# Rows of the output projection parked in DRAM, two more weight buffers, and row sums on GpSimd

## The chip, the cores and the metric

One NeuronCore of a Trainium2 chip runs the whole kernel; times are device microseconds of that core, median of three runs. TensorE (PE) multiplies, VectorE (DVE), ScalarE (ACT) and GpSimd (POOL) do the rest, and the queue of SyncE (SP) issues nearly all DMAs.

## The reference

A block of one layer over 512 tokens of width 1024: three mixers (gated linear attention, stick-breaking attention, pooling) share one input and one output projection, then a mixture of 32 experts (two per token, all in one group of eight), then a gated input embedding and a last norm.

```
h = x + mix @ w_out
h = h + hier_moe(rmsnorm(h), ...)          # 32 experts of 3 x 1 MB, 2 per token
gate = sigmoid(rmsnorm(h, g3) @ ple_gate_w + ple_gate_b)
h = h + gate * (p @ ple_proj_w)
return rmsnorm(h, final_norm_g)
```

## The kernel before

The 512 tokens are four tiles of 128. After the mixers, `h1[t]` holds the rows of the output projection (x plus mix times w_out), one buffer of 128x1024 floats for each tile, in the pool `hp`; they stay in SBUF to the end. Routing makes for every token two places in lists of experts; the normed rows go to `tnd` in DRAM, and each of 16 steps gathers the rows of two experts (`xg`), turns them, multiplies by gate and up weights (`gate_up`, line 997), then by the down weights (`down`, line 1029), and scatters the results to `yd` in DRAM by an indirect DMA of GpSimd. Only the last step, 15, stays on the chip: `scatter` adds its rows to `h1` by a matmul with a one-hot matrix (line 1051) and an addition on VectorE (line 1053).

Weights come in 96 units of 1 MB, issued in a fixed order by SP (`load_units`, line 691) into buffers that a list `ring` hands out: 20 in all, each given back when its step has used it. A load also waits for the one issued three before it (`AHEAD`). SP, PE and, from step 14 on, ACT and DVE run in the order in which the code is written; GpSimd's order is set by the scheduler of the framework.

Behind the units SP issues, for the tail: the returned rows of tile 0 (`load_y(0)`, both experts' rows, 1 MB), four pieces of the gate weights (`gate_load`, 4 MB), `load_y(1)`, a broadcast row of 0.5 MB, `load_y(2)`, another such row, `load_y(3)`. Then, for each tile t:

- `add_y(t)` (line 1164): two additions of 128x1024 of the returned rows to `h1[t]`, and `scatter` of step 15's; together `sums(t)`.
- `turn(t)` (line 1221): eight transposes on PE, copies by ACT (1223) and DVE (1224), as a high and a low part.
- `gate(t)`: 48 matmuls of 128x512 (line 1242) with the gate weights, which `gate_hi` (ACT, 1071) and `gate_lo` (DVE, 1075) have split in 16 pieces into a high and a low part.
- `rms(t)`: squares on ACT (1229), two tiny sums on DVE (1208, 1210), and a power on GpSimd (`rsp`, line 63).
- `finish(t)`: DVE 1252 (which needs `rsp`), ACT sigmoid 1253, DVE 1254, 1255, 1257, ACT 1256, and the output DMA.

ACT and DVE hold the copies of `turn(t+1)` behind the first half of `finish(t)`. 32 small steps of the embedding's product (`ple`, line 724) are spread over the expert steps by the table `PLE`, the last twelve over the tail by `PLE_LAST`.

Of the kernel before, what the change touches and what calls it, by code (L numbers as in the profile page):

```python
# [27 lines left out]

FILL = (8, 3, 0, 1, 0, 1, 0, 1, 0, 1, 1, 1, 4, 2, 2, 2, 9)

PLE = (5, 1, 1, 1, 1, 1, 1, 1, 1, 1, 1, 1, 1, 1, 2)
PLE_LAST = (4, 4, 4)
AHEAD = 3
NR, NL = 4, 9
CLEAR = (7, 8, 9, 10)
# [53 lines left out]
def mixers(ctx, tc, A, K, dbg):  # L89
# [360 lines left out]
    sbctx.close()  # L450
    pctx.close()
    hp = ctx.enter_context(tc.tile_pool(name="hp", bufs=1, side="left"))
    h1 = K["h1"] = [hp.tile([P, D], F32, name=f"h1_{t}") for t in range(NT)]
    for t in range(NT):
        nc.sync.dma_start(h1[t], A["x"][t * P:(t + 1) * P, :])
    parts = (step for t in range(NT) for hf in range(2) for step in out_proj(nc, K, mixh, mixl, hf, t, WO_EARLY))
# [157 lines left out]
def ffn(ctx, tc, A, K, mixh, mixl, out, dbg, stage):  # L614
# [67 lines left out]

    slab, loads = {}, []

    def load_units(m=96):

        while ring and m and len(slab) < 96:
            n, m = len(slab), m - 1
            n = n - n % 6 + (0, 3, 1, 4, 2, 5)[n % 6]
            slab[n] = unit(F32, [P, 2048])  # L690
            loads.append(nc.sync.dma_start(slab[n], A["w_exp"][n // 3, n % 3]).ins)
            if len(loads) > AHEAD:
                tc.add_manual_dep(loads[-1], loads[-1 - AHEAD].name,
                                  mybir.DependencyInfo(mybir.DependencyClass.Sync, mybir.DependencyReason.DATA))
# [20 lines left out]
    def ple_steps():  # L715

        pT, pW = pl_in
        for j in range(8):
            t, hf = j // 2, j % 2
            p = ps("pe", "sc" if j < 5 else "gu")  # L720
            for c in range(2):
                for k in range(2):
                    n = hf * 512 + c * 256
                    PE.matmul(p[:, c * 256:c * 256 + 256], pT[:, k * S + t * P:k * S + (t + 1) * P], pW[:, k, n:n + 256],  # L724
                              start=(k == 0), stop=(k == 1))
                    if c == k == 1:
                        kept.append((t, hf, p))
                        ple_out()
                    yield
# [14 lines left out]
    V.tensor_copy(cm.rearrange("p a b -> p (a b)"), cmf)  # L744
    V.tensor_tensor(rw, rw, g2c[:, :, None].to_broadcast([P, KC, 36]), ALU.mult)
    tnd = dram.tile([S, D], F32, name="tnd")
    Ab = mw.tile([P, NT, 32], BF, name="Ab")
    pr_ = cw.tile([P, 448], F32, name="pr", tag="cmf")
    posA = pr_[:, :128].rearrange("p (t e) -> p t e", t=NT)
# [87 lines left out]
    def weights(t, g8, e8, id2, c0):  # L837
# [22 lines left out]
        V.tensor_copy(rt(1), pe(c0))  # L860
        V.tensor_tensor(rt(2), pe(c0), rt(1), ALU.subtract)

    chosen = {}
    halves = [(t, hf) for t in range(NT) for hf in range(2)]

# [7 lines left out]
    with tc.manual_schedule(engines={mybir.EngineType.PE}):  # L873
        for hf in range(2):
            part(hf, 0, WO_LATE[:2])
        for n in range(len(halves) - 1):
            part(halves[n][1], halves[n][0], WO_LATE[2:] if n < 2 else WO_LATE)
            if n >= 2:
                logits(*halves[n - 2])
            if n >= 1:  # L880
                route_in(*halves[n - 1])
            if n >= 2:
                t, hf = halves[n - 2]
                if hf:
                    run(route(t))
                    load_units(2)
                    if t > 0:
                        position(t - 1)
                        run(weights(t - 1, *chosen[t - 1]))
                elif t > 1:  # L890
                    position(t - 1)
                    run(weights(t - 1, *chosen[t - 1]))
        with tc.manual_schedule(engines={mybir.EngineType.DVE}):
            last_part = out_proj(nc, K, mixh, mixl, 1, NT - 1, WO_LATE)
            run(last_part, 2)
            logits(NT - 2, 1)
            steps = [route(t) for t in (NT - 2, NT - 1)]
            run(steps[0], 7)
            run(last_part)
        ring.extend(((mix, "m3"), (mix, "m1"), (mix, "m2")))  # L900
        for hf in range(2):
            route_in(NT - 1, hf)
        logits(NT - 1, 0)
# [28 lines left out]
    def one_hot(i, t):  # L932

        if t == 0:
            Dm[i] = mw.tile([P, NT, 2, 64], BF, name="Dm", tag="Dm")
        V.tensor_tensor(Dm[i][:, t], iota64[:, None, :].to_broadcast([P, 2, 64]),
                        posA[:, t, 2 * i:2 * i + 2, None].to_broadcast([P, 2, 64]), ALU.is_equal)
# [120 lines left out]
    def gate_load(j):  # L1058
        gr.append(unit(F32, [P, 4, 512]))
        nc.sync.dma_start(gr[j], A["ple_gate_w"][j])  # L1060
# [16 lines left out]
            free(gr[2 * hf + k // 4])  # L1077

    order.enter_context(tc.manual_schedule(engines={mybir.EngineType.PE}))
    load_units(1)  # L1080
    with tc.manual_schedule(engines={mybir.EngineType.DVE}):
        run(steps[0])
        for t in (0, 1):
            hot_rms(t)
        logits(NT - 1, 1)
        run(steps[1], 3)
        position(NT - 2)
        spread(0)
        run(steps[1], 2)
        hot_rms(NT - 2)  # L1090
        spread(1)
        run(steps[1])
        spread(2)
        position(NT - 1)
        hot_rms(NT - 1)
        for t in range(3):
            one_hot(1, t)
        spread(NT - 1)
        for hf in range(2):
            gather_T(0, hf)  # L1100
        one_hot(1, NT - 1)
    ple_load()
    load_units()

# [56 lines left out]
    def add_y(t, rs=(0, 1)):  # L1161

        for r in rs:
            V.tensor_tensor(h1[t], h1[t], ys[t][:, r], ALU.add)  # L1164

    def load_y(t):
        ys.append(unit(F32, [P, 2, D]))
# [3 lines left out]
    for i in range(16):  # L1171
# [18 lines left out]
        if i == 14:  # L1190
            load_y(0)
            for j in range(4):
                gate_load(j)
            load_y(1)
            rows = mix.tile([P, 2, D], F32, name="rows", tag="m0")
            nc.sync.dma_start(rows[:, 0], bcast(A["ple_gate_b"]))
            load_y(2)
            nc.sync.dma_start(rows[:, 1], bcast(A["final_norm_g"]))
            load_y(3)


# [72 lines left out]
    def tail(sums=None):  # L1274

        for t in range(NT):
            at = {}
            if t + 1 < NT:
                at[1, 1] = lambda: prep(t + 1)
            if sums and t == 0:  # L1280
                at[0, 6] = lambda: sums(1)
            if sums and t + 2 < NT:
                at[1, 5] = lambda: sums(t + 2)
            last(t, at)

    def sums(t):
        add_y(t)
        for hf in range(2):
            scatter(2 * t + hf)

    down(15, lambda n: n < 2 and add_y(0, (n,)))
    ple(PLE_LAST[0])
    gate_hi(0, 0)
    for hf in range(2):
        scatter(hf)
    gate_lo(0, 0)
    gate_hi(1, 0)
    ple(PLE_LAST[1])
    lo = [turn(0, hf) for hf in range(2)]
    ple(PLE_LAST[2])  # L1300
    free(pl_in[1])
    for f in lo:
        f()
    gate_lo(1, 0)
    for k in range(2, KC):
        gate_hi(k, 0)
        gate_lo(k, 0)
    count_beyond()
    for k in range(KC):
        gate_hi(k, 1)  # L1310
        gate_lo(k, 1)
    ov_slots = ring[:3]
    junk, h3s = (unit(F32, shape, slot) for shape, slot in zip(([P, 2, 512], [P, 4, 512]), ring[3:]))
    SC.preload_act_table_set("sigmoid_and_others")
    rms(0)
    tail(sums)
    ends.close()
# [157 lines left out]
```

## Time and profile before

| | |
|---|---|
| median of 3 runs | 556.58 us (556.06 to 557.71) |
| the profiled execution | 556.99 us, its span 555.2 us |
| PE busy | 514.5 us (93%) |
| DVE / ACT / POOL busy | 276.2 / 210.8 / 87.1 us |
| moved by DMA | 148.82 MB, mean 268 GB/s |

The span is that from the first to the last instruction; 1.8 us of the execution lie outside it. The mean hides stages: the mixers fill the first 170 us, the output projection and routing go to 241 us, the expert steps to 477 us, and the tail to the end.

### The profile page before, as it was taken

The numbers are of one execution on the slowest core, as the hardware profiler recorded it, in microseconds if no ns is written. First come the engines' busy times: TensorE is split into PE (matmuls) and PEld (weight loads), VectorE is DVE, ScalarE is ACT, GpSimd is POOL, SyncE is SP. The second block draws the span as 40 slices with busy tenths as digits, with TensorE's granted clock in tenths as the row PEclk, the third lists the DMA queues.
The fourth block names the chain that finished last, engine by engine and source line by source line (L and its number), as shares of the span: only waits on it lengthen the run. The fifth ranks groups of instructions, "written<-read, shape, count | busy, mean of one in ns | idle before, by whom it ended". The sixth has DMA issues, their size and how long they took to land.

```text
span 555.2 us, 7581 instructions
## 1 busy us (share of the span) xinstructions
PE 514.5 (93%) x2713; PEld 325.3 (59%) x2713; DVE 276.2 (50%) x735; ACT 210.8 (38%) x443; POOL 87.1 (16%) x122
## 2 busy tenths in 40 slices
PE   8899999999999999999999999998798987949992
PEld 5797886876997788844333333332233332638872
DVE  6762957756747565773422322221121111597764
ACT  7466665646766434411112111110111101473352
POOL 3301111221008500002111111111110000011110
PEclk9999999999999999999999999999999999988997
DMA  8882222300339669989999999999999999950111
GB/s 303 265 325 73 62 72 71 91 26 2 117 126 418 251 263 413 348 337 387 416 412 417 399 394 387 375 383 396 368 399 418 416 418 390 416 211 0 40 44 73
DMA packets 35641, 148.82 MB, mean 268 GB/s; under 512 B 6557, under 2 KB 14109, under 8 KB 22160
## 3 DMA queue, kind: packets, MB, share of 16 engines
q1 hardware_dynamic: 29984, 137.46, 64.3%
q0 software_dynamic: 4320, 7.95, 3.8%
q10 hardware_dynamic: 1296, 2.89, 1.3%
q8 instruction: 23, 0.38, 0.3%
q14 instruction: 18, 0.15, 0.1%
HBM read 139.61 MB, written 16.25 MB: 281 GB/s over the span
## 4 chain that ended last, share of the span: by engine, by line
PE 62%; DMA 18%; DVE 9%; ACT 7%; issue 2%; POOL 1%; SPq 0%; ACTq 0%; DVEq 0%; POOLq 0%
DMA unit<-in_w_exp_dram 17%; PE gu L997 12%; PE pj L234 9%; PE po L80 8%; PE dn L1029 7%; PE pj L257 5%; PE z L257 4%; PE z L311 2%; PE po L333 2%; PE pe L724 2%; ACT unit L1071 2%; PE x L974 1%; DVE h L1164 1%; PE pl L780 1%; PE z L292 1%
## 5 line engine op out<-in xcount | busy, mean ns | idle before, releaser
L997 PE MATMUL gu<-unit,xT 128*64 128x512 f32 x512 | 127.5, 598 | 13.1 <-DMA unit<-in_w_exp_dram 13.1
L997 PEld LDWEIGHTS gu<-unit,xT 128*64 128x64 f32 x512 | 37.0, 137 | 85.0 <-issue 59.2
L1029 PE MATMUL dn<-unit,hidT 128*64 128x512 f32 x256 | 60.6, 599 | 1.7 <-ACT hidT L1020 0.8
L234 PE MATMUL pj<-xh,wp 128*128 128x512 f32 x176 | 51.2, 398 | 0.4 <-ACT wp L69 0.4
L1242 PE MATMUL pg<-unit 128*128 128x512 f32 (+1 forms) x216 | 47.9, 378 | 0.8 <-ACT unit L735 0.6
L1002 ACT ACTIVATE sg<-gu 128x256 f32<-128x256 f32 x16 | 6.1, 383 | 110.5 <-PE gu L997 110.5
L1003 DVE SCALAR_TENSOR_TENSOR hid<-sg,wsl,gu 128x256 f32<-128x256 f32 x16 | 7.7, 478 | 79.6 <-ACT sg L1002 79.5
L1242 PEld LDWEIGHTS pg<-unit 128*128 128x128 f32 x216 | 37.9, 193 | 9.0 <-ACT unit L735 0.7
L1043 POOL DMA_INDIRECT yd<-big,idy x15 | 15.1, 1009 | 163.8 <-ACT big L1033 163.8
L1029 PEld LDWEIGHTS dn<-unit,hidT 128*64 128x64 f32 x256 | 19.7, 137 | 32.0 <-issue 24.2
L234 PEld LDWEIGHTS pj<-xh,wp 128*128 128x128 f32 x176 | 32.6, 188 | 8.2 <-ACT wp L69 1.3
L1033 ACT ACTIVATE big<-dn 128x512 f32<-128x512 f32 x30 | 17.9, 597 | 50.0 <-PE dn L1029 50.0
L930 DVE COPY SL<-sl 128x10 f32<-128x10 f32 (+1 forms) x17 | 2.8, 167 | 66.0 <-PE sl L929 66.0
L70 DVE TENSOR_TENSOR wp<-wraw,wp 128x768 fp32r<-128x768 f32 (+2 forms) x28 | 25.8, 927 | 13.6 <-ACT wp L69 13.4
L69 ACT ACTIVATE wp<-wraw 128x768 fp32r<-128x768 f32 (+2 forms) x28 | 22.8, 817 | 20.2 <-PE pj L234 9.8
L234 PE MATMUL pj<-xl,wp 128*128 128x512 f32 x88 | 29.4, 401 | 0.0
L986 DVE TENSOR_TENSOR xT<-xt,g2c 128x512 f32<-128x512 f32 x30 | 20.6, 687 | 11.8 <-PE xt L985 11.7
L80 PE MATMUL po<-wo,mx 128*128 128x512 f32 x96 | 25.7, 408 | 0.0
L257 PE MATMUL pj<-wp,xh 128*128 128x384 f32 x96 | 24.8, 351 | 0.0
L80 PE MATMUL po<-unit,mx 128*128 128x512 f32 x96 | 24.1, 399 | 0.0
L943 POOL DMA_INDIRECT xg<-tnd,idx x15 | 15.4, 1029 | 33.7 <-issue 16.0
L985 PEld LDWEIGHTS xt<-ident,xg 128*128 128x128 f32 x120 | 13.4, 141 | 11.5 <-issue 11.4
(293 smaller groups left out, 881.2 us busy)
## 6 DMA issues: line engine op xcount, KB each, us to landing
unit<-in_w_exp_dram SPq DMA_DIRECT2D x96, 1024.0 KB, 8.7
wraw<-in_w_in_dram SPq DMA_DIRECT2D x20, 384.0 KB, 3.5
yd<-zero SPq DMA_DIRECT2D x4, 1024.0 KB, 7.9
unit<-yd SPq DMA_DIRECT2D x4, 1024.0 KB, 6.5
unit<-in_ple_gate_w_dram SPq DMA_DIRECT2D x4, 1024.0 KB
wraw<-in_w_out_dram SPq DMA_DIRECT2D x8, 256.0 KB, 3.0
h<-in_x_dram SPq DMA_DIRECT2D x4, 512.0 KB
unit<-in_w_out_dram SPq DMA_DIRECT2D x4, 512.0 KB, 7.8
```

The costliest lines, as they stand in the source:

```text
L69: nc.scalar.activation(h, src, AF.Copy)
L70: nc.vector.tensor_tensor(l, src, h.bitcast(F32), ALU.subtract)
L80: nc.tensor.matmul(p, a[k][:, ts_], K["wo"][k][:, b, hs], start=(n == 0), stop=(n == 3 * len(ks) - 1))
L234: PE.matmul(q, a[:, i * P:(i + 1) * P], b[k], start=(n == 0), stop=(n == 3 * KC - 1))
L257: PE.matmul(p[t][:, :W_IN[j]], a[k][:, t * P:(t + 1) * P], b, start=(n == 0), stop=(n == 3 * KC - 1))
L943: G.indirect_dma_start(out=xg[i % 2], out_offset=None, in_=tnd, in_offset=bass.IndirectOffsetOnAxis(ap=idx[:, i:i + 1], axis=0), bounds_ch ...
L986: V.tensor_tensor(xTs[i, hf], p.rearrange("p (a b) -> p a b", a=4), g2c[:, 4 * hf:4 * hf + 4, None].to_broadcast([P, 4, P]), ALU.mult)
L997: PE.matmul(gu[64 * e:64 * e + 64], xTs[i, k // 4][:, k % 4, 64 * e:64 * e + 64], w[e][k // 4][:, 512 * (k % 4):512 * (k % 4) + 512], star ...
L1029: PE.matmul(dn[64 * e:64 * e + 64], hT[:, f, 64 * e:64 * e + 64], w[e][2][:, 1024 * f + 512 * hf:1024 * f + 512 * hf + 512], start=(f == 0 ...
L1033: SC.activation(o[:, 512 * hf:512 * hf + 512], dn, AF.Copy)
L1043: G.indirect_dma_start(out=yd, out_offset=bass.IndirectOffsetOnAxis(ap=idy[:, i:i + 1], axis=0), in_=o, in_offset=None, bounds_check=2 * S ...
L1242: PE.matmul(p, hT[t][:, a, ks], gw[k][:, b, hs], start=start and n == 0, stop=stop and n == len(ab) - 1)
```

## The change

`h1` becomes two buffers of two tiles each. `store_h(t)` writes each tile's rows to `hd` in DRAM, on SP's queue between loads of units (the first two tiles during routing, the last two after it). When the rows have been used, the two buffers join `ring`, so that 22 buffers serve the units. `load_h(t)` brings the rows back: tile 0 just ahead of the last two units (tile 1 shares its buffer), tiles 1, 2 and 3 ahead of the returned rows of the same tile. `add_y` of tiles 1 to 3 runs on GpSimd. Eight steps of `ple` move from the tail into the expert steps; the ACT table for the sigmoid is loaded during step 15's `down`; tile 1's `sums` moves from inside tile 0's gate into the splitting of the gate weights.

```diff
-PLE = (5, 1, 1, 1, 1, 1, 1, 1, 1, 1, 1, 1, 1, 1, 2)
-PLE_LAST = (4, 4, 4)
+PLE = (5, 1, 1, 1, 1, 1, 2, 2, 2, 2, 2, 2, 2, 2, 2)
+PLE_LAST = 4
...
-    h1 = K["h1"] = [hp.tile([P, D], F32, name=f"h1_{t}") for t in range(NT)]
+    K["hp"] = hp
+    hh = [hp.tile([P, 2, D], F32, name=f"h1_{j}", tag=f"h{j}") for j in range(2)]
+    h1 = K["h1"] = [hh[t // 2][:, t % 2] for t in range(NT)]
...
+    def load_h(t):
+
+        if t % 2 == 0:
+            back.append(unit(F32, [P, 2, D]))
+        h1[t] = back[-1][:, t % 2]
+        nc.sync.dma_start(h1[t], hd[t * P:(t + 1) * P, :])
...
         while ring and m and len(slab) < 96:
+            if len(slab) == 94 and not back:
+                load_h(0)
+                continue
...
+    def store_h(t):
+        nc.sync.dma_start(hd[t * P:(t + 1) * P, :], h1[t])
...
                     load_units(2)
+                    store_h(t)
...
-    load_units(1)
+    load_units(3)
+    for t in (NT - 2, NT - 1):
+        store_h(t)
...
+    ring.extend(((K["hp"], "h0"), (K["hp"], "h1")))
     ple_load()
     load_units()
...
-            V.tensor_tensor(h1[t], h1[t], ys[t][:, r], ALU.add)
+            (G if t else V).tensor_tensor(h1[t], h1[t], ys[t][:, r], ALU.add)
...
+            load_h(1)
             load_y(1)
             rows = mix.tile([P, 2, D], F32, name="rows", tag="m0")
             nc.sync.dma_start(rows[:, 0], bcast(A["ple_gate_b"]))
+            load_h(2)
             load_y(2)
             nc.sync.dma_start(rows[:, 1], bcast(A["final_norm_g"]))
+            load_h(3)
             load_y(3)
...
-            if sums and t == 0:
-                at[0, 6] = lambda: sums(1)
             if sums and t + 2 < NT:
+                at[0, 0] = lambda: add_y(t + 2)
                 at[1, 5] = lambda: sums(t + 2)
             last(t, at)
 
     def sums(t):
-        add_y(t)
         for hf in range(2):
             scatter(2 * t + hf)
 
-    down(15, lambda n: n < 2 and add_y(0, (n,)))
-    ple(PLE_LAST[0])
+    def behind_down(n):
+        if n == 0:
+            SC.preload_act_table_set("sigmoid_and_others")
+        if n < 2:
+            add_y(0, (n,))
+
+    down(15, behind_down)
+    ple(PLE_LAST)
     gate_hi(0, 0)
     for hf in range(2):
         scatter(hf)
     gate_lo(0, 0)
     gate_hi(1, 0)
-    ple(PLE_LAST[1])
     lo = [turn(0, hf) for hf in range(2)]
-    ple(PLE_LAST[2])
     free(pl_in[1])
+    add_y(1)
...
     for k in range(KC):
         gate_hi(k, 1)
+        if k == 2:
+            sums(1)
         gate_lo(k, 1)
+    count_beyond()
     ov_slots = ring[:3]
     junk, h3s = (unit(F32, shape, slot) for shape, slot in zip(([P, 2, 512], [P, 4, 512]), ring[3:]))
-    SC.preload_act_table_set("sigmoid_and_others")
```

GpSimd's queue behind the last scatter to `yd` (L1043 before, L1062 now); `rsp` and `rsl` are the powers of the two norms. Before:

```order
L1043 DMA yd<-big,idy 1024x1024 x2
L63 TENSOR_TENSOR rsp<-ms,mhalf 128x1 x2
L63 TENSOR_TENSOR rsl<-ms,mhalf 128x1
L63 TENSOR_TENSOR rsp<-ms,mhalf 128x1
L63 TENSOR_TENSOR rsl<-ms,mhalf 128x1
L63 TENSOR_TENSOR rsp<-ms,mhalf 128x1
```

And of the change:

```order
L1062 DMA yd<-big,idy 1024x1024 x2
L1186 TENSOR_TENSOR unit<-unit 128x1024 x4
L63 TENSOR_TENSOR rsp<-ms,mhalf 128x1
L1186 TENSOR_TENSOR unit<-unit 128x1024 x2
L63 TENSOR_TENSOR rsp<-ms,mhalf 128x1
L63 TENSOR_TENSOR rsl<-ms,mhalf 128x1
```

The four additions for tiles 1 and 2 now stand ahead of tile 0's `rsp`, the two for tile 3 ahead of tile 1's.

VectorE's queue, from tile 0's sums with step 15 (L1053 before, L1072 now) to the second half of the turned tile 1 (L1224, now L1249). Before:

```order
L1075 SCALAR_TENSOR_TENSOR unit<-unit,g3c 128x512 x7
L1136 CAST on<-pov 1x1
L1075 SCALAR_TENSOR_TENSOR unit<-unit,g3c 128x512 x8
L1208 TENSOR_SCALAR ms<-pm 128x1
L1210 SCALAR_TENSOR_TENSOR ms<-pm,ms 128x1
L1164 TENSOR_TENSOR h_1_1509<-h_1_1509,unit 128x1024 x2
L1053 TENSOR_TENSOR h_1_1509<-h_1_1509,sc 128x512 x2
L1252 SCALAR_TENSOR_TENSOR unit<-pg,rsp,rows 128x512
```

And of the change (L1094 is `gate_lo`, L1233 and L1235 the sums of `rms`, L1277 the first line of `finish`):

```order
L1094 SCALAR_TENSOR_TENSOR unit<-unit,g3c 128x512 x9
L1072 TENSOR_TENSOR unit<-unit,sc 128x512 x2
L1094 SCALAR_TENSOR_TENSOR unit<-unit,g3c 128x512 x6
L1158 CAST on<-pov 1x1
L1233 TENSOR_SCALAR ms<-pm 128x1
L1235 SCALAR_TENSOR_TENSOR ms<-pm,ms 128x1
L1277 SCALAR_TENSOR_TENSOR unit<-pg,rsp,rows 128x512
```

Tile 1's sum with step 15, which needs GpSimd's additions, now stands ahead of six of the sixteen `gate_lo` and of tile 0's `rms`.

SP's queue behind the last but two of the units, before and now (`hd` is the DRAM copy of the rows):

```order
L691 DMA unit<-in_w_exp_dram 128x2048 x80
L1168 DMA unit<-yd 128x2x1024
L1060 DMA unit<-in_ple_gate_w_dram 128x2048 x4
L1168 DMA unit<-yd 128x2x1024
L1196 DMA rows<-in_ple_gate_b_dram 128x1024
L1168 DMA unit<-yd 128x2x1024
```

```order
L692 DMA unit<-hd 128x1024
L705 DMA unit<-in_w_exp_dram 128x2048 x2
L1190 DMA unit<-yd 128x2x1024
L1079 DMA unit<-in_ple_gate_w_dram 128x2048 x4
L692 DMA unit<-hd 128x1024
L1190 DMA unit<-yd 128x2x1024
L1219 DMA rows<-in_ple_gate_b_dram 128x1024
L692 DMA unit<-hd 128x1024
L1190 DMA unit<-yd 128x2x1024
```

Half a megabyte of `hd` stands ahead of the last two units, and half a megabyte ahead of each later tile's returned rows.

## Rows read from the trace of the kernel before

**Rows 1.** The page, busy tenths of 16 DMA engines in 40 slices.

```profile
DMA  8882222300339669989999999999999999950111
```

**Rows 2.** Stretches: length; PE, PEld, DVE, ACT, POOL busy; PE clock, DMA share, GB/s.

```profile
226.00:230.00 4.00, 4.00 (x24) 3.31 (x23) 2.61 (x15) 0.57 (x2) 0.00 (x0) 1.00 0.78 258
...
244.00:248.00 4.00, 4.00 (x21) 1.18 (x18) 3.44 (x19) 1.84 (x7) 1.24 (x1) 1.00 0.55 184
...
362.00:467.00 105.00, 90.90 (x400) 34.35 (x396) 17.84 (x69) 13.10 (x27) 12.11 (x12) 1.00 1.01 401
```

**Rows 3.** Timeline of SP at the end: start us, us, what was issued.

```profile
468.27 0.38 SPq L1168 DMA_DIRECT2D unit<-yd  x1
...
474.75 0.33 SPq L1198 DMA_DIRECT2D rows<-in_final_norm_g_dram  x1
```

**Rows 4.** DMA issues of the same two: KB, us from issue to landing.

```profile
unit<-yd SPq DMA_DIRECT2D x1, 1024.0 KB, 6.5
...
rows<-in_final_norm_g_dram SPq DMA_DIRECT2D x1, 512.0 KB, 18.4
```

**Rows 5.** Timeline of PE in the tail; in brackets idle time before, and its end.

```profile
476.74 2.00 PE L724 MATMUL pe<-unit,big 128*128 128x256 f32 x8
...
489.87 2.24 PE L1242 MATMUL pg<-unit 128*128 128x512 f32 x9
...
499.29 1.97 PE L1221 MATMUL xt<-ident,h 128*128 128x128 f32 x8 [7.18 <-DVE h L1053]
...
505.91 8.50 PE L1242 MATMUL pg<-unit 128*128 128x512 f32 x36
...
533.41 11.76 PE L1242 MATMUL pg<-unit 128*128 128x512 f32 x72 [0.23 <-ACT unit L1223]
```

**Rows 6.** Timeline of DVE and ACT in the tail.

```profile
474.75 1.23 DVE L1164 TENSOR_TENSOR h<-h,unit 128x1024 f32<-128x1024 f32 x1 [2.57 <-DMA unit<-yd]
...
489.32 5.37 DVE L1075 SCALAR_TENSOR_TENSOR unit<-unit,g3c 128x512 fp32r<-128x512 f32 x8
...
493.23 1.28 ACT L1314 ACT_TABLE_LOAD   x1
...
495.96 2.48 DVE L1164 TENSOR_TENSOR h<-h,unit 128x1024 f32<-128x1024 f32 x2
...
498.54 1.29 DVE L1053 TENSOR_TENSOR h<-h,sc 128x512 f32<-128x512 f32 x2
...
499.75 0.74 DVE L1252 SCALAR_TENSOR_TENSOR unit<-pg,rsp,rows 128x512 f32<-128x512 f32 x1
...
503.39 1.07 ACT L1223 ACTIVATE unit<-xt 128x512 fp32r<-128x512 f32 x2
```

**Rows 7.** Stretches of the tail with PE's granted clock, columns as in rows 2.

```profile
490.00:500.00 10.00, 2.82 (x14) 2.09 (x13) 8.82 (x15) 5.83 (x11) 1.48 (x1) 0.84 0.34 136
500.00:510.00 10.00, 10.00 (x40) 8.29 (x40) 8.22 (x14) 3.55 (x9) 1.47 (x1) 0.82 0.00 0
```

**Rows 8.** Timeline of POOL and DVE where both work; last, one tiny power.

```profile
16.13 2.04 POOL L183 TENSOR_TENSOR gs<-gs,xr 128x512 f32<-128x512 f32 x1 [2.07 <-ACT xr L181]
...
16.94 1.78 DVE L179 SCALAR_TENSOR_TENSOR xl<-xr,g,xh 128x512 fp32r<-128x512 f32 x1
...
168.12 1.85 POOL L382 TENSOR_TENSOR gs<-gs,gng 128x384 f32<-128x384 f32 x1 [17.43 <-DVE sig L367]
...
168.56 0.55 DVE L367 SCALAR_TENSOR_TENSOR sig<-gs,tmp 128x384 f32<-128x384 f32 x1
...
171.01 1.01 POOL L382 TENSOR_TENSOR gs<-gs,gng 128x384 f32<-128x384 f32 x1
...
175.14 2.38 POOL L677 TENSOR_TENSOR unit<-unit 128x1024 fp32r<-128x1024 f32 x1
...
513.51 0.54 POOL L63 TENSOR_TENSOR rsl<-ms,mhalf 128x1 f32<-128x1 f32 x1 [6.10 <-DVE ms L1210]
```

**Rows 9.** Instructions of line 179: shortest, median, longest in ns.

```profile
L179 DVE SCALAR_TENSOR_TENSOR xl<-xr,g,xh x5: 741/752/1780, 10.0 to 16.9; 128x512 fp32r<-128x512 f32 x5
```

More of the change, by code (lines that the diff above doesn't have):

```diff
@@ L683, in ffn @@
     slab, loads = {}, []
+    def load_h(t):
[3 more added lines that the diff above has]
+        nc.sync.dma_start(h1[t], hd[t * P:(t + 1) * P, :])
+    back = []
     def load_units(m=96):
         while ring and m and len(slab) < 96:
+            if len(slab) == 94 and not back:
+                load_h(0)
+                continue
             n, m = len(slab), m - 1
@@ L719, in ple_steps @@
             t, hf = j // 2, j % 2
-            p = ps("pe", "sc" if j < 5 else "gu")
+            p = ps("pe", "sc" if j < 7 else "gu")
             for c in range(2):
@@ L746, in ffn @@
     tnd = dram.tile([S, D], F32, name="tnd")
+    hd = dram.tile([S, D], F32, name="hd")
     Ab = mw.tile([P, NT, 32], BF, name="Ab")
@@ L1307, in ffn @@
         gate_lo(k, 0)
-    count_beyond()
     for k in range(KC):
         gate_hi(k, 1)
+        if k == 2:
+            sums(1)
         gate_lo(k, 1)
+    count_beyond()
     ov_slots = ring[:3]
     junk, h3s = (unit(F32, shape, slot) for shape, slot in zip(([P, 2, 512], [P, 4, 512]), ring[3:]))
-    SC.preload_act_table_set("sigmoid_and_others")
     rms(0)
```

## The prediction

> **What bounds the kernel now.** I read the page's slices first: from the 16th slice of 40 to the 35th the DMA engines are at 80% or more, mostly at 90 [rows 1]. The stretches say what that means. From 362 to 467 us the DMA share is 1.01 while PE works 90.9 of 105 us, so the stream of expert units sets the pace [rows 2]. Only in two places while units stream are the DMA engines short of work: 226 to 230 (0.78) and 244 to 248 (0.55), where loads wait for buffers [rows 2]. So more buffers can win back 0.22 x 4 + 0.45 x 4 = 2.7 us and no more; behind them the stream is bound by bytes.
>
> Then the tail's timeline. The returned rows of tile 0 are issued at 468.27 and land 6.5 us later, at 474.8; VectorE's addition waits for exactly that [rows 3, 4, 6]. PE finishes tile 0's first half of gates at 489.87 + 2.24 = 492.1 and then stands 7.18 us, until VectorE has added step 15's rows to tile 1 (L1053), which queues behind the last `gate_lo`, `rms(0)` and `add_y(1)` [rows 5, 6]. During the wait its clock falls: 0.84 and 0.82 mean 3.2 + 3.6 = 6.8 us at the lower of its two levels (1.2 GHz), from 496.8 to 503.6; the 4.3 us of it behind the wait cost half of themselves, 2.1 us [rows 7]. From 505.91 on 36 matmuls take 8.50 us, and the last 72 start at 533.41 with 0.23 us of waiting: PE is then busy to the end [rows 5]. Nine of the 36 are still tile 0's, so tile 1 begins at 505.91 + 9 x 0.236 = 508.0. The end of the kernel moves with that moment, and I compute it for the change.
>
> **The unit stream.** Price of a half megabyte: from 474.8 (tile 0's rows) to 474.75 + 18.4 = 493.2 (the second broadcast row) the queue moved 4 gate pieces, tile 1's and 2's rows and two half rows, 7 MB in 18.4 us: 2.63 us a megabyte, 1.31 a half [rows 3, 4]. Four stores cost 5.3 us in a stream without slack. They and the two extra loads fill the two gaps, 2.7. Net: units 2.6 us later. Bounds: stores hidden entirely (they write, the rest reads), 2.7 earlier; gaps not filled, 5.3 later. I take the sum, because a share of 1 leaves nowhere to hide a copy. (The last store needs tile 3's rows, and behind it on SP stand the loads that fill the second gap; if it is late, the gap stays, which is that bound.) `load_h(0)` delays what comes behind it by another 1.3. Tile 0's returned rows then land at 474.8 + 3.9 = 478.7. Behind them: 4 MB of gates, half a megabyte of h1, 1 MB of tile 1's rows, 5.5 x 2.63 = 14.5, so **tile 1's rows land at 493.2** (before: 474.8 + 5 x 2.63 = 488.0); tile 2's, 2 MB on, at 498.5; tile 3's, 2 MB on, at 503.8.
>
> **What is taken off the tail.** Eight `ple` steps, two groups like that of 2.00 us, are 3.8 to 4 us of PE [rows 5]; in the expert steps they are hidden by PE's 14 us of waiting from 362 to 467, and those that fall before 362 only delay a PE that waits later; without that cover they would cost their 4 us again [rows 2]. The table load is 1.28 on ACT, `add_y(1)` 2.48 on VectorE [rows 6]. All three shorten the way to the 499.29 transposes, but a later landing takes their place: tile 0's first addition starts 3.9 later, which eats the `ple` steps, and tile 1 now waits for its rows.
>
> **What GpSimd makes of it.** One 128x1024 addition of two SBUF operands takes it 2.38 us alone [rows 8]; `add_y(1)` is two, 493.2 to 498.0. Half an L1053 pair is 0.65 [rows 6], so tile 1's transposes start at about 498.6 instead of 499.29. 0.7 us won, no more.
>
> VectorE has meanwhile stopped: that L1053 stands ahead of six `gate_lo`, which before were done by 494.7 and now start at 499.3. Six take 6 x 0.67 = 4.0 [rows 6]. Behind them are a cast and `rms(0)`'s two tiny sums (0.4, an estimate: before, the sums and their wait for ACT fit into the 1.3 us from 494.7 to 495.96 [rows 6]), then `rsp(0)` on GpSimd (0.54, as its twin `rsl` [rows 8]), then `finish(0)`. And from 498.5, when tile 2's rows are there, GpSimd runs the two additions of `add_y(2)`, which its queue has ahead of `rsp(0)`.
>
> Do the two engines get in each other's way? The trace shows it: line 179 on VectorE, two SBUF operands, takes 741 to 752 ns and 1780 when a GpSimd addition runs [rows 8, 9]; that addition (16.13 to 18.17) ends 0.55 before it. At 168.12 the GpSimd multiply takes 1.85 where the next takes 1.01, while VectorE's two-operand line 367 inside it keeps its 0.55 [rows 8]. So they take turns, and a whole instruction's worth is lost. `gate_lo` has the form of line 179. From 498.5 on there are 2 x 2.38 + 4.0 = 8.8 us to be done in turn: 507.3, plus 0.4 and 0.5, **rsp(0) done at 508.2**. Without such turns it is 503.3 + 0.9 = 504.2.
>
> The Trainium skill, page "SBUF — State Buffer", section "Who interferes with whom", calls this an exclusive lock: whoever issues first holds it for the whole instruction and the other fully blocks, and a VectorE instruction meets it only with two SBUF inputs against a GpSimd instruction that reads SBUF. The trace agrees in the 1780 ns of line 179. Taken strictly, turn by turn, the rule puts every GpSimd addition between two VectorE instructions, and tile 1 below starts at 515.7; by the row at 168.56, where VectorE kept its turn for a second instruction, it starts at 513.3.
>
> From L1252 to the ACT copy of the turned tile 1 it is 503.39 - 499.75 = 3.64 us, the copy's half 0.54 [rows 6]: tile 1 starts 4.2 after `rsp`, at 512.4. But `add_y(3)` follows `rsp(0)` on GpSimd (rows there since 503.8) and meets L1254 and L1255, both of two SBUF operands: the first addition ends 2.38 after `rsp`, some 0.9 after L1254 wants to start; the second costs 2.4 more if it gets between. **Tile 1 at 513.3 to 515.7**, 5.3 to 7.7 late. PE has then stood from about 506 to 514, as long as the wait that lowered its clock before, so 0 to 2.1 us of half speed come on top.
>
> Nothing gives it back: tiles 1 and 2 are PE's own 25.4 us, from 508.0 to 533.41 [rows 5], which VectorE's saved 2.48 a tile does not shorten. The sum is 5.3 to 7.7 for the late start and 0 to 2.1 for the clock, so 5.3 to 9.8; I take +7, somewhat below the middle, since the strict turns and the whole loss of clock are the far ends. The profiled execution's 556.99 (span 555.2, and 1.8 outside of it) would be 564.0; it lies 0.4 above the median 556.58, so 563.5.
>
> **Rivals.**
>
> *No turns on the port, the same time.* `rsp(0)` at 504.2, tile 1 at 508.4, +0.4: 557. For it: at 168.56 VectorE went on undisturbed. Against: 1780 ns [rows 9]. It also needs that GpSimd is nowhere late. A stream late by 1 us less makes it 556.
>
> *Faster: the stores cost nothing and the head start stays.* Then everything behind lands 5.3 us earlier than I have it, tile 1's rows at 487.9 and its transposes at 493.3; PE waits about a microsecond, keeps its clock, and with free engines tile 1 starts at 503, 5 early: 551.6. With half of that (2.6) and no turns, 554.4. It decides when PE's 7.18 us of waiting [rows 5] shrinks below 3 and `rsp(0)` ends before 502. Against: a DMA share of 1.01 [rows 2], and six `gate_lo` still behind the sum.
>
> *The buffers do nothing.* That the two units help little is part of my sum: the stretches allow 2.7, the stores take 5.3. If loads waited for buffers all the way, PE's waits from 362 on would end on slots, not landings; DMA at 1.01 says otherwise.
>
> **How the numbers follow.** A median cannot be told from the old one within 0.3%, 1.7 us. Engines in turns, late rows: 0.67, 559 to 568 (5.3 to 9.8, the bounds of the stream taken off or put on in part). No turns: 0.18, 555 to 558.3. Faster: 0.15, 551 to 554.9. Each case can also end a little outside its own range, which a few in a hundred of the first and second do to both sides. So slower 0.67, same 0.18, faster 0.15; the range 555.2 to 567.5 leaves out the faster case and the last few in a hundred on top, two in ten.
>
> **What would show it.** Right: DMA share near 1 at 244 to 248; the last unit's matmuls some 2.6 later than 467; GpSimd's additions from about 493, four in a row, VectorE's L1053 for tile 1 ending its longest wait "POOL"; `gate_lo` of 3 us beside GpSimd's additions; tile 1's ACT copy after 511; a second stretch of lower clock near 506 to 515. Wrong: additions that start before 490, `gate_lo` at 0.74 throughout, or `rsp(0)` before 503. What would upset it most is the landing of tile 1's and tile 2's rows, which no row shows alone: I have it from a mean rate. If pieces land in another order than they were issued, GpSimd's times move with them.

## The result, and the profile after

The change takes 559.5 us (median of 20 runs) where before takes 556.16: a ratio of 1.0057, 95% interval 1.0043 to 1.0071, or 3.2 us slower. The forecast said slower, 563.5, within 555.2 to 567.5: the sign and the range hold, the size of +7 is more than twice what was measured. The profiled execution took 559.58, its span is 557.8.

The tail after, first SP and VectorE in the timeline (start, length, engine, line, operation, in brackets the idle time before):

```profile
469.34 0.38 SPq L1190 DMA_DIRECT2D unit<-yd  x1
```

```profile
475.68 1.23 DVE L1186 TENSOR_TENSOR unit<-unit 128x1024 f32<-128x1024 f32 x1 [4.82 <-DMA unit<-yd]
...
482.50 6.05 DVE L1094 SCALAR_TENSOR_TENSOR unit<-unit,g3c 128x512 fp32r<-128x512 f32 x9
494.49 1.28 DVE L1072 TENSOR_TENSOR unit<-unit,sc 128x512 f32<-128x512 f32 x2 [5.94 <-POOL unit L1186]
495.69 7.75 DVE L1094 SCALAR_TENSOR_TENSOR unit<-unit,g3c 128x512 fp32r<-128x512 f32 x6
503.37 0.14 DVE L1158 CAST on<-pov 1x1 int32<-1x1 f32 x1
...
507.42 2.77 DVE L1280 TENSOR_TENSOR unit<-unit 128x512 f32<-128x512 f32 x1
```

Tile 0's returned rows are there at 475.7, not at 478.7 as I had it. VectorE stops for 5.94 us ahead of tile 1's sums, and the six `gate_lo` behind them take 7.75 us. The group of line 1094 in the stretch from 495 to 510 (shortest, median, longest in ns) shows one of 2824 where the median is 737; instruction by instruction it is the first two that wait, 2354 and 2824:

```profile
L1094 DVE SCALAR_TENSOR_TENSOR unit<-unit,g3c x6: 737/737/2824, 495.7 to 502.7; 128x512 fp32r<-128x512 f32 x6
```

GpSimd's timeline shows for what: the additions of tile 2, and for line 1280 those of tile 3.

```profile
489.70 4.76 POOL L1186 TENSOR_TENSOR unit<-unit 128x1024 f32<-128x1024 f32 x2 [27.48 <-DMA rows<-in_ple_gate_b_dram]
495.15 5.09 POOL L1186 TENSOR_TENSOR unit<-unit 128x1024 f32<-128x1024 f32 x2 [0.70 <-issue]
503.92 0.57 POOL L63 TENSOR_TENSOR rsp<-ms,mhalf 128x1 f32<-128x1 f32 x1 [3.68 <-DVE ms L1235]
504.47 5.16 POOL L1186 TENSOR_TENSOR unit<-unit 128x1024 f32<-128x1024 f32 x2
```

PE's timeline, and stretches with its granted clock (columns as in rows 2):

```profile
482.73 6.50 PE L1267 MATMUL pg<-unit 128*128 128x512 f32 x27
495.23 1.12 PE L1246 MATMUL xt<-ident,unit 128*128 128x128 f32 x4 [6.00 <-DVE unit L1072]
503.56 1.11 PE L1246 MATMUL xt<-ident,unit 128*128 128x128 f32 x4 [7.21 <-DVE ms L1233]
504.33 4.46 PE L1267 MATMUL pg<-unit 128*128 128x512 f32 x12
...
509.56 8.80 PE L1267 MATMUL pg<-unit 128*128 128x512 f32 x36
...
531.94 16.40 PE L1267 MATMUL pg<-unit 128*128 128x512 f32 x93
```

```profile
226.00:230.00 4.00, 4.00 (x31) 3.68 (x30) 2.51 (x12) 1.21 (x3) 0.00 (x0) 1.00 0.99 414
244.00:248.00 4.00, 4.00 (x24) 1.54 (x24) 3.33 (x22) 2.14 (x7) 1.24 (x1) 1.00 1.02 430
492.00:496.00 4.00, 0.77 (x4) 0.72 (x4) 1.51 (x3) 0.00 (x0) 3.23 (x3) 0.73 1.02 418
...
504.00:508.00 4.00, 4.00 (x14) 3.24 (x13) 2.69 (x3) 0.63 (x1) 3.92 (x3) 0.56 0.00 2
```

PE waits twice where before it waited once for 7.18 us [rows 5]: 6.00 for tile 1's sums, then 7.21 between the two halves of the transposes. The second half needs the PSUM tile of the count's product (`pov`), whose cast now stands behind the six `gate_lo` (the bracket names L1233, the instruction next to the cast; cast_early below shows that it is the cast). Tile 1's first product starts at 511.6, against 508.0; PE ends at 548.3, against 533.41 + 11.76 = 545.2 [rows 5], 3.2 us later.

This pair's 3.2 us are not all the change's doing. The start varies from execution to execution: SP issued unit 6 at 198.99 after (shown further down) and before at

```profile
197.46 0.33 SPq L691 DMA_DIRECT2D unit<-in_w_exp_dram  x1
```

and anywhere from 197.1 to 201.7 in the 16 profiles of this case; the first product of line 257 starts between 24.8 and 28.9 in them, and between before and after it already differs by the 1.5 us of unit 6. So below I count from unit 6 (the units numbered from 0 in the order of their issue): tile 1's first product is 310.5 us behind it before and 312.7 after, the end of PE 347.7 and 349.4. This pair of profiles shows 1.6 to 2.2 us of the 3.2 by which the medians differ. So the ratios below, of many runs, decide what a part of the change costs, and the profiles show where.

### The profile page after: what moved, and what is told of

Read it like the earlier page. It is cut to its first block, busy times and chain, and to the rows that moved or that the text cites. A ratio compares the mean times of both kernels' runs of the same rounds, so it can differ in the third digit from the quotient of the medians.

```text
span 557.8 us, 7607 instructions
## 1 busy us (share of the span) xinstructions
PE 515.1 (92%) x2713; PEld 326.2 (58%) x2713; DVE 275.6 (49%) x729; ACT 210.8 (38%) x443; POOL 99.2 (18%) x128
## 4 chain that ended last, share of the span: by engine, by line
PE 58%; DMA 33%; DVE 5%; ACT 2%; issue 1%; POOL 0%; SPq 0%; DVEq 0%; POOLq 0%; ACTq 0%
DMA unit<-in_w_exp_dram 26%; PE pj L234 9%; PE po L80 8%; PE gu L1016 7%; PE pg L1267 6%; PE pj L257 5%; PE z L257 4%; PE dn L1048 3%; DMA unit<-yd 3%; PE z L311 2%; PE po L333 2%; DMA unit<-in_ple_gate_w_dram 2%; DMA xg<-tnd,idx 1%; DVE unit L1094 1%; PE x L993 1%; PE pl L795 1%
## 5 line engine op out<-in xcount | busy, mean ns | idle before, releaser
L1062 POOL DMA_INDIRECT yd<-big,idy x15 | 15.1, 1009 | 164.4 <-ACT big L1052 164.4
L257 PE MATMUL pj<-wp,xh 128*128 128x384 f32 x96 | 24.8, 351 | 0.0
```

The costliest lines, as they stand in the source:

```text
L257: PE.matmul(p[t][:, :W_IN[j]], a[k][:, t * P:(t + 1) * P], b, start=(n == 0), stop=(n == 3 * KC - 1))
L1062: G.indirect_dma_start(out=yd, out_offset=bass.IndirectOffsetOnAxis(ap=idy[:, i:i + 1], axis=0), in_=o, in_offset=None, bounds_check=2 * S ...
```

## The experiments

Theory A: the parking pays for itself, and the loss is in the tail, where VectorE stands still ahead of six `gate_lo` and then takes turns with GpSimd. Its rival, theory B, is the forecast's first term: stores and loads make the stream of units late, and the rows with it. Narrower rivals are named where they are tested.

Each label is a kernel with part of the change, or an edit of the change or of before. Ratios are to runs of before on the same chip, which had medians of 556.08 to 557.2. The last two columns are from each profile, in us behind unit 6: the issue of unit 93, and tile 1's first product of its gate.

| run | ratio (95%) | unit 93 | tile 1 |
|---|---|---|---|
| before | | 260.4 | 310.5 |
| the change | 1.0057 (1.0043 to 1.0071) | 259.2 | 312.7 |
| parking_alone | 0.9996 (0.9971 to 1.0021) | 261.0 | 310.3 |
| tail_alone | 1.0056 (1.0029 to 1.0084) | 261.2 | 313.3 |
| stores_alone | 1.0015 (0.9993 to 1.0038) | 260.0 | 309.3 |
| stores_late | 1.0117 (1.0092 to 1.0141) | 266.1 | 316.2 |
| buffers_without_stores | 1.0031 (1.0003 to 1.0059) | 258.0 | 312.4 |
| cast_early | 1.0059 (1.0032 to 1.0085) | 259.3 | 313.1 |
| power_before_tile2 | 1.0015 (0.9986 to 1.0043) | 258.8 | 309.3 |
| additions_on_vector | 0.9987 (0.9963 to 1.0010) | 258.3 | 306.5 |
| sums_after_split | 0.9970 (0.9945 to 0.9994) | 259.2 | 308.6 |
| additions_vector_after_split | 0.9944 (0.9925 to 0.9962) | 258.9 | 305.0 |
| tile1_ahead | 0.9971 (0.9942 to 1.0001) | 259.6 | 299.7 |
| tail_reordered | 0.9996 (0.9964 to 1.0027) | 258.8 | 297.9 |
| tail_reordered_no_parking | 0.9993 (0.9970 to 1.0016) | 261.0 | 299.7 |
| tail_reordered_gpsimd | 0.9994 (0.9975 to 1.0013) | 258.3 | 298.8 |

**The two halves of the change.** parking_alone is the change with the old tail (tables, table load, `sums` with `add_y` on VectorE inside, tile 1's at `at[0, 6]`, that is ahead of the seventh of the eight steps of tile 0's first half of gates).

> The stores, the two buffers and the loads back as in the change; the tail (ple steps, table load, place and engine of the sums) as before. Theory A (the parking pays for itself, the loss is in the order of the tail on VectorE and GpSimd): within 1.5 us of before, tile 0's returned rows at about 474 to 476 as before, VectorE's gate_lo at 0.67 each, no longer. Theory B (my forecast's term: the stores make the stream late by 2.6 us, load_h(0) by 1.3 more): 2.6 to 4 us slower than before, tile 0's rows landing near 478.7.

tail_alone is before with the new tail only; `h1` stays four buffers in SBUF, no `store_h`, no `load_h`.

> The tail's edits alone (ple steps earlier, table load in step 15, additions of tiles 1 to 3 on GpSimd, tile 1's sums ahead of six gate_lo); no parking: rows stay in SBUF, 20 buffers, the loads as before. Theory A: 2 to 4 us slower than before, six gate_lo of 1.2 us and more beside add_y(2), tile 1's first copy on ACT at 509 to 511. Theory B: since the rows are not late, GpSimd's additions start early enough: within 1 us of before or faster.

Parking costs nothing that shows (0.2%, 1.2 us, at the edge of its interval); the tail alone costs 0.56% of the change's 0.57%. Theory B, my forecast's term for the stream, is out; so are its late rows. The trace of tail_alone has the turns as well: the first three of its six `gate_lo` take 1.62, 2.82 and 2.83 us.

**What a store costs.** stores_alone adds to before the four stores at the change's places:

```diff
+    def store_h(t):
+        nc.sync.dma_start(hd[t * P:(t + 1) * P, :], h1[t])
...
                     load_units(2)
+                    store_h(t)
...
-    load_units(1)
+    load_units(3)
+    for t in (NT - 2, NT - 1):
+        store_h(t)
```

> The kernel before with the four stores of 0.5 MB on SP's queue at the change's places and nothing else: the copy is never read, the buffers stay 20. Theory B (a stream without slack): 2.6 us slower where they fill the two gaps, up to 5.3 where they don't. Theory A: the stream of before loses time to waits for buffers also where its DMA share reads 1.0 (VectorE and PE free a buffer later than the queue wants one, from 300 to 372), so stores take 1 to 3 us at most, because a load that waits for a buffer is not held up by a store in front of it.

Measured: +0.8 us at the middle, 2.1 at the edge of the interval. buffers_without_stores is the change without them. It reads the rows back from `x`, so it leaves the mixers' part out of them; only its times are of use:

```diff
-        nc.sync.dma_start(h1[t], hd[t * P:(t + 1) * P, :])
+        nc.sync.dma_start(h1[t], A["x"][t * P:(t + 1) * P, :])
...
-                    store_h(t)
...
-    for t in (NT - 2, NT - 1):
-        store_h(t)
```

> The change without its four stores; the rows brought back are read from x instead of the copy, so that the mixers' part is missing in them; all else, the two buffers too, as in the change. Theory A (slack of the stream lies in loads that wait for buffers, 7.7 us between 300 and 372 before, 2 in the change): the stores do cost something once the buffers are there: unit 93 is issued 1 to 4 us sooner after unit 6 than the change's 259.2, and the kernel is 1 to 3.5 us faster than the change. Theory E (stores are hidden altogether, writes beside reads): unit 93 at 259 as in the change, time the same within 0.7 us.

By the two middles it is 1.4 us faster than the change (the intervals meet), and SP's timeline shows where the price goes. Units 6, 22 and 93 of the change, then of buffers_without_stores:

```profile
198.99 0.33 SPq L705 DMA_DIRECT2D unit<-in_w_exp_dram  x1
...
254.68 0.33 SPq L705 DMA_DIRECT2D unit<-in_w_exp_dram  x1
...
458.21 0.33 SPq L705 DMA_DIRECT2D unit<-in_w_exp_dram  x1
```

```profile
199.43 0.33 SPq L705 DMA_DIRECT2D unit<-in_w_exp_dram  x1
...
250.04 0.33 SPq L705 DMA_DIRECT2D unit<-in_w_exp_dram  x1
...
457.47 0.33 SPq L705 DMA_DIRECT2D unit<-in_w_exp_dram  x1
```

At unit 22 the stores have made the stream late by 55.7 - 50.6 = 5.1 us, close to the 5.3 of the forecast. At unit 93 1.2 are left. stores_late puts the same stores in before where nothing follows that could make them up:

```diff
+        if i in (9, 10):
+            for t in (2 * i - 18, 2 * i - 17):
+                nc.sync.dma_start(hd[t * P:(t + 1) * P, :], h1[t])
```

> As stores_alone, but the four stores stand on SP's queue behind units 73 and 79 (two each, issued near 405 and 421 us), where loads no longer wait for buffers but only for earlier loads, and PE waits for units. Theory A (the early stores are made up by loads that would have waited for buffers): here nothing makes them up, 3 to 5.3 us slower than before, unit 93 issued 3 to 5 us later after unit 6. Theory E (writes are hidden beside reads): within 1.5 us of before, as stores_alone.

Units 6 and 93 of stores_late:

```profile
198.15 0.33 SPq L691 DMA_DIRECT2D unit<-in_w_exp_dram  x1
...
464.23 0.33 SPq L691 DMA_DIRECT2D unit<-in_w_exp_dram  x1
```

1.0117 is 6.5 us, more than the 3 to 5.3 that I expected, and unit 93 comes 5.7 later than in before (unit 95, the last, 4.6): Theory E is out. The same four stores cost 4.6 to 6.5 us where PE waits for units; issued early they cost 5.1 at unit 22 and 1.2 at unit 93, so there the stream makes most of it up. The expectations of stores_alone and of buffers_without_stores place waits for buffers between 300 and 372 us, and that is wrong: in before loads wait for PE to free a buffer for about 16 us in all from 226 to 275, and for 0.4 from 300 to 372. How the stream makes up the rest, between 275 and 400 us, the runs don't show. There the share of the DMA engines reads 0.97 to 1.01 in before and they move 380 to 414 GB/s; from 420 on it reads 1.02 at 417 and more.

```profile
340.00:360.00 20.00, 19.81 (x102) 7.73 (x100) 5.17 (x17) 3.21 (x7) 2.02 (x2) 1.00 0.97 380
...
440.00:460.00 20.00, 17.38 (x79) 7.28 (x76) 2.55 (x9) 3.21 (x7) 1.01 (x1) 1.00 1.02 419
```

**What the tail loses.** The five runs here are edits of the change. cast_early puts the count ahead of the second half of the splitting again:

```diff
+    count_beyond()
     for k in range(KC):
         gate_hi(k, 1)
...
         gate_lo(k, 1)
-    count_beyond()
```

> The change, with the count's product and its cast back at their place ahead of the second half of the splitting. In the change the second half of tile 1's transposes waits for that cast's PSUM tile until 503.56. Theory A (finish(0) with rsp(0) sets ACT's copy of the turned tile 1): PE goes on at 496.4 instead of 503.6 and only waits later, for the copy at 510.9: within 0.7 us of the change. Theory D (PE's wait for the cast sets tile 1): PE is through with tile 0 by 504 and tile 1 starts 3 to 6 us earlier, 3 to 6 us faster than the change.

The same time as the change: with the cast out of the way PE goes on, and waits 6.16 us for ACT's copy instead. PE's timeline in cast_early:

```profile
493.77 1.97 PE L1246 MATMUL xt<-ident,unit 128*128 128x128 f32 x8 [5.10 <-DVE unit L1072]
...
510.48 7.99 PE L1267 MATMUL pg<-unit 128*128 128x512 f32 x27 [6.16 <-ACT unit L1248]
```

So the wait for the cast, which I had overlooked, hides behind the one that I had: `rsp(0)`, finish(0), then the copy.

power_before_tile2 gives GpSimd the order of the code:

```diff
-    rms(0)
-    tail(sums)
+    with tc.manual_schedule(engines={mybir.EngineType.Pool}):
+        rms(0)
+        tail(sums)
```

> The change, with GpSimd's instructions of the tail in the order of the code: tile 0's rsp ahead of the additions for tile 2. Theory A (turns on the port, then rsp): beside the six gate_lo there is nothing left on GpSimd, so they are done at 499.8 instead of 503.4, rsp(0) at 500.9 instead of 504.5; finish(0) then meets add_y(2) and loses 0.7 to 2.4 again; tile 1's first copy at 506 to 508 instead of 510.9: 2.5 to 4.5 us faster than the change, level with before. Theory C (no turns; six gate_lo behind the sums are the whole loss): they take 7.7 us as in the change, and nothing is won, within 1 us.

By the middles it wins 1.0057 - 1.0015, 2.3 us, just under the 2.5 expected (the intervals just meet); tile 1 starts 3.4 us sooner. Theory C is out: VectorE's timeline shows that the six `gate_lo` take 4.06 us again, and that finish(0) meets the additions instead (L1280):

```profile
494.56 4.06 DVE L1094 SCALAR_TENSOR_TENSOR unit<-unit,g3c 128x512 fp32r<-128x512 f32 x6
...
502.58 2.76 DVE L1280 TENSOR_TENSOR unit<-unit 128x512 f32<-128x512 f32 x1
```

So a turn costs VectorE up to 2.1 us (L1280 takes 0.69 where no addition runs), and moving the additions moves part of the loss to finish(0). additions_on_vector takes them off GpSimd:

```diff
-            (G if t else V).tensor_tensor(h1[t], h1[t], ys[t][:, r], ALU.add)
+            V.tensor_tensor(h1[t], h1[t], ys[t][:, r], ALU.add)
...
-                at[0, 0] = lambda: add_y(t + 2)
...
     def sums(t):
+        add_y(t)
...
-    add_y(1)
```

> The change, but add_y of tiles 1 to 3 on VectorE, directly ahead of step 15's sums of the same tile, which stand where the change has them (tile 1's ahead of six gate_lo). Theory A: one addition is 1.23 instead of 2.38 us and nothing takes turns: tile 1's sums done at about 493.2, the six gate_lo at 497.2, rsp(0) at 498.3, tile 1's products from about 504 instead of 511.7: 5 to 7 us faster than the change, 2 to 4 faster than before. Theory B, or a loss that comes from the place of the sums alone: VectorE's 5.0 us of additions more for the later tiles and six gate_lo behind the sums keep it at the change's time, within 1.5 us.

3.9 us faster than the change, not 5 to 7, and level with before. Tile 1 did start 6.1 us earlier, and PE ended 5.1 earlier; 0.8 of the difference is a wait for ACT's copy ahead of tile 3. That VectorE's additions for the later tiles are behind it is likely, not shown. sums_after_split leaves them on GpSimd and moves tile 1's sums:

```diff
-        if k == 2:
-            sums(1)
         gate_lo(k, 1)
     count_beyond()
+    sums(1)
```

> The change, with tile 1's sums (and no GpSimd order given) behind all sixteen gate_lo and the count's cast instead of ahead of the last six. Theory A: the six begin at 488.5 and take turns with add_y(1): done by 495.5 to 497, the cast and rms(0) follow at once, rsp(0) behind only the first addition of tile 2 at about 498; tile 1 from 505 to 507 instead of 511.7: 4 to 6 us faster than the change, 1 to 3 faster than before. Rival (only the total of VectorE's and GpSimd's work counts, not its order): within 1 us of the change.

4.8 faster than the change, as expected, and a little faster than before. additions_vector_after_split has both of the last two edits.

> The change with both edits: additions on VectorE (as additions_on_vector) and tile 1's sums behind all gate_lo and the cast (as sums_after_split). If the two lose the same time, that is VectorE standing still ahead of the six gate_lo and its turns with GpSimd: 555 as either of them, ratio to before 0.995 to 0.999. If they add up: 551 to 553, ratio 0.990 to 0.994.

Between the two answers, with an interval that reaches into both: 1.0057 - 0.9944 is 6.3 us, more than either edit alone and less than their sum of 8.7. They are largely but not wholly the same loss, VectorE standing still or taking turns. This version beats before by 3.1 us and the change by 6.3. PE's timeline, and two stretches, the second that in which the clock was at 0.82 before [rows 7]:

```profile
497.35 1.25 PE L1246 MATMUL xt<-ident,unit 128*128 128x128 f32 x8 [3.62 <-DVE unit L1072]
```

```profile
486.00:496.00 10.00, 7.73 (x28) 5.84 (x27) 9.96 (x16) 7.22 (x14) 0.00 (x0) 0.86 1.02 394
...
500.00:510.00 10.00, 10.00 (x44) 8.09 (x44) 8.06 (x13) 3.77 (x10) 1.48 (x1) 1.00 0.01 2
```

PE waits 3.62 us instead of 13.2, and behind this wait the clock is at its upper level. It is not so all through this execution: from 482 to 488 the granted clock is 0.50 while PE works on tile 0, and from 532 to 538, behind a wait of 2.28 us ahead of tile 3, it reads 0.79, 0.50 and 0.86. This execution took 557.33, 2.9 us above the median of this version, so its trace shows the version at its slowest.

**Further, and no further.** tile1_ahead adds to this: for tile 0 all 48 products stand ahead of tile 1's transposes, ACT's and VectorE's copies of these ahead of finish(0), tile 2's sums between its halves.

```diff
+        if at.get("ahead"):
+            for j, (hf, c, n, p) in enumerate(pieces):
+                products(j, p, slice(hf * 512 + c, hf * 512 + c + n))
+            at["ahead"]()
+            products = lambda j, p, hs: j and sums(t + 2)
         finish(t, pieces, products)
```

> The parking as in the change; additions on VectorE; tile 1's sums behind all gate_lo; for tile 0 all 48 products stand ahead of tile 1's transposes, and ACT's and VectorE's copies of these ahead of finish(0). By Theory A PE's wait for tile 1 shrinks from 13.2 us to 2 or 3 (rows at 489.4, sums at 496.4, copies at 498): tile 1 starts at about 499 to 500 once the first PSUM tile of tile 0 is read, with a further wait of 1 to 2 us for the second; 8 to 11 us faster than the change and 5 to 8 faster than before. If something else than this wait bounds the tail (bytes, or ACT and VectorE in all four tiles), 2 us or less.

tail_reordered does so for tiles 1 and 2, with `prep(t + 1)` of the later tiles still at (1, 1), ahead of the second step of the second half; the other two are its variants without parking, and with `(G if t > 1 else V)` in `add_y`.

> As tile1_ahead, and for tiles 1 and 2 as well all products of a tile stand ahead of its finish on VectorE and ACT, so that the copies of the next turned tile no longer queue behind it, and the sums of the tile after next stand between the two halves of finish. In tile1_ahead PE began tile 1 as early as expected, but waited 1.9, 2.5 and 2.3 us in tiles 1 to 3, each time for VectorE's sums or ACT's copy. Theory A: these 6.7 us go down to 1 or 2: 5 to 8 us faster than before, 8 to 11 faster than the change. If VectorE is the bound of the tail by its total work (about 11.8 of 13 us a tile), 2 us or less over tile1_ahead.

> The tail of tail_reordered with the DMA of before: rows stay in SBUF, 20 buffers, no copies. If the parking is worth what the unit stream shows in the profiles (unit 93 issued 1 to 2 us sooner after unit 6 with it), 0.5 to 1.5 us slower than tail_reordered; if the parking is worth nothing, the same; by my forecast's term (stream 2.6 late, rows 3.9 late), 2 to 4 us faster than tail_reordered.

> tail_reordered with the additions of tiles 2 and 3 on GpSimd (its order left to the scheduler). Theory A (an addition on GpSimd holds the port 2.38 us where VectorE needs 1.23, and VectorE's two-operand instructions wait in turn): VectorE loses beside each pair of additions 2 to 4 us in finish(0) and the turned copies, more than the 2.48 it is spared: 1 to 4 us slower than tail_reordered. If the work taken off VectorE counts: 1 to 3 faster.

No forecast of theory A came out. Tile 1 starts 11 to 13 us earlier than before, as worked out, and by the ratios the end comes 0.2 to 1.6 us sooner, and each of the four intervals still has no gain at all within it. PE's timeline in tail_reordered, and its clock:

```profile
494.25 1.25 PE L1246 MATMUL xt<-ident,unit 128*128 128x128 f32 x8 [0.85 <-DVE unit L1072]
...
504.61 1.26 PE L1246 MATMUL xt<-ident,unit 128*128 128x128 f32 x8 [1.91 <-DVE unit L1072]
...
520.23 1.72 PE L1246 MATMUL xt<-ident,unit 128*128 128x128 f32 x8 [2.08 <-DVE unit L1072]
```

```profile
518.00:520.00 2.00, 0.15 (x1) 0.00 (x0) 1.86 (x3) 0.00 (x0) 0.00 (x0) 1.00 0.00 0
520.00:522.00 2.00, 1.77 (x9) 1.59 (x10) 1.44 (x3) 0.53 (x1) 0.00 (x0) 0.66 0.00 0
522.00:524.00 2.00, 2.00 (x6) 1.52 (x6) 1.80 (x3) 0.46 (x2) 0.00 (x0) 0.50 0.00 0
```

PE now waits for VectorE's sums in each later tile, and after 2.08 us of the last wait its clock falls too; finish(2) holds VectorE and ACT until 538, so that all of finish(3) but its first instruction is left behind PE's end. PE ends at 539.1, and ACT's last scaling starts at 547.24, 8.1 us later; in the change these are 548.3 and 552.16, 3.8. So 4.3 us of what PE won are lost again in the chain of VectorE and ACT. That is not the whole account: counted from unit 6 this execution still ends 3.3 us sooner than before's, and the medians differ by 0.2. tail_reordered_no_parking takes the same time as tail_reordered (0.9993 and 0.9996): with this tail, too, the parking is worth nothing, neither a gain nor a loss. On GpSimd the additions of tiles 2 and 3 neither gain nor lose: PE waits 4.28 us for tile 2's sums instead of 1.91, and not at all for tile 3's.

## Why the prediction was right or wrong

**The step that failed** is the unit stream: "Net: units 2.6 us later", and with it "`load_h(0)` delays what comes behind it by another 1.3", tile 0's rows at 478.7. Counted from unit 6, I had the rows' issue 3.9 us later than before; it is 0.5 earlier (469.34 - 198.99 against 468.27 - 197.46 [rows 3]), 4.4 from the forecast. The price of a store was right, 5.1 of 5.3 at unit 22. Wrong was "a share of 1 leaves nowhere to hide a copy": the stores are issued from 213 to 233 us, the last some 145 us ahead of PE's first wait of half a microsecond for a unit (378.2), and 4 of the 5 us are made up on the way, at a share near 1 all the time. And `load_h(0)` delays nothing behind it: `load_y(0)` waits for the scatter of step 14 to land, 3.9 us before and 5.7 in the change (SP's waits: us in all, times, longest):

```profile
SPq L1168 <- DMA yd<-big,idy: 3.9, 1, 3.9
```

```profile
SPq L1190 <- DMA yd<-big,idy: 5.7, 1, 5.7
```

The prediction's own sign of being wrong, "additions that start before 490", came: 489.70.

**Two buffers, 2.7 us**: right in size. Without the stores unit 93 comes 2.4 us sooner than before, and about 3 sooner than in the two other kernels with 20 buffers and no stores (261.2, 261.0). With the stores the two gaps are full, shares of 0.99 and 1.02; without them the first still reads 0.86 and the second 1.01. A single profile tells such a time only to 1 us or so: parking_alone, with buffers and stores, had 261.0 where the change had 259.2.

**GpSimd's additions and the turns**: right. Two additions take 4.76; from the end of tile 1's to the last `gate_lo` it was 9.0 us (494.46 to 503.44), forecast 9.3 (498.0 to 507.3). `rsp(0)` was done 14.8 us after tile 1's rows (489.70 to 504.49), forecast 15.0 (493.2 to 508.2). From there to tile 1's first product it was 7.2, forecast 5.1 to 7.5: both of tile 3's additions got between, as in the strict turns. The page "SBUF — State Buffer" of the Trainium skill, section "Who interferes with whom", calls the shared port pair an exclusive lock and lets the order of issue decide who blocks; the 2824 ns of `gate_lo` agree. In sums_after_split (last section) four `gate_lo` that start behind an addition run ahead of it, which that order would not give. The page's section also counts VectorE's 2-port modes as a cause, which the prediction's "only" leaves out.

**Tile 1 at 513.3 to 515.7**: from unit 6 315.8 to 318.2. Taking off the 4.4 by which the stream was misjudged leaves 311.4 to 313.8, and 312.7 was measured. The clock, 0 to 2.1 on top, came to 0.4 at most: the low level lasts longer (0.73 from 492 to 496, 0.56 from 504 to 508, 0.50 between), but PE stands in most of it. It works for about 1.1 + 4.0 us there, which cost half of themselves, 2.5, against 2.1 before. It may have cost nothing: in cast_early PE has done this work earlier, stands 6.16 us for ACT's copy, and tile 1 starts no sooner.

**What I did not see** is the PSUM tile of the cast; it costs nothing only because ACT's copy is later still.

**The rivals.** "No turns" fell by the 7.75 us. "Faster: the stores cost nothing and the head start stays" was right in its first half: the rows are no later. It fell because `rsp(0)` did not end before 502 and PE's wait grew instead of shrinking. "The buffers do nothing" fell by the 2.4 us above.

## What to carry to other kernels

Work given to GpSimd is not simply taken off VectorE if both read two SBUF operands: here two additions of 2.34 and 2.67 us there held up two `gate_lo` by 1.6 and 2.1, and VectorE does such an addition in 1.23. A copy costs its bytes where it stands, but in this stream most of that was gone again by the time PE waited for it: price a copy at that wait, not at its own place. And when one engine's wait is removed, work out the end from every engine that comes after it: 11 us and more won at tile 1 were worth 0.2 to 1.6 at the end.

## What the runs showed of the hardware

GpSimd does not always get its turn. In sums_after_split its first addition starts at 488.23 beside a run of `gate_lo` and takes 5028 ns, while VectorE's go on at 746, the last four of them started after it (groups of both lines from 484 to 500):

```profile
L1186 POOL TENSOR_TENSOR unit<-unit x4: 2337/2366/5028, 488.2 to 498.6; 128x1024 f32<-128x1024 f32 x4
```

```profile
L1094 DVE SCALAR_TENSOR_TENSOR unit<-unit,g3c x11: 744/746/747, 483.7 to 490.3; 128x512 fp32r<-128x512 f32 x11
```

In the change, with the same two instructions, they alternate. What decides it the runs don't show. VectorE's L1072, with one operand in PSUM, is not held up: in sums_after_split a pair of them stands wholly inside an addition (495.63 to 497.99) and takes the usual 1.29.

```profile
495.70 1.29 DVE L1072 TENSOR_TENSOR unit<-unit,sc 128x512 f32<-128x512 f32 x2 [4.59 <-POOL unit L1186]
```

The start of the kernel scatters by more than the change is worth. In the five profiles without the two buffers unit 6 is issued at 197.2 to 198.2, in the eleven with them at 197.1 to 201.7; whether the buffers have a part in that is open.
